# One projection stage of a hybrid transformer trunk: small loads issued at other places, and the third batch of triangular systems solved beside 12 token tiles of the second sweep

## The chip, the cores and the metric

The kernel runs on one core of one Trainium2 chip, as one launch. The metric is the device time of that launch in microseconds. Three executions of the kernel before took 3792.86, 3789.95 and 3793.18 us, median 3792.86 us. Names of engines in this text: PE is TensorE's matmul, PEld its weight load, DVE is VectorE, ACT is ScalarE, POOL is GpSimd, and SP is SyncE, whose instruction queue issues nearly all DMAs here.

## The reference, cut to what matters

One layer for 256 prompt tokens and 2048 latent tokens (18 tiles of 128 tokens together). The input `h` is normalised and modulated, and one projection of it feeds three groups of heads: A (attention with normalised and rotated q and k), B (a gated DeltaNet in chunks of 64 tokens, in both directions) and C (neighbourhood attention). Then follow an output projection and a SwiGLU FFN.

```python
def latent_mixer(h, ka_ctx, va_ctx, s_ctx, kc_ctx, vc_ctx, w_in, g_qk_a, ...):
    a_q, a_k, a_v, b_qkv, b_g, b_beta, b_alpha, c_q, c_k, c_v = split_projection(h @ w_in)
    qa = axial_rope(rmsnorm(a_q.reshape(b, L, A_HEADS, HEAD_DIM), g_qk_a[0]))
    ka = axial_rope(rmsnorm(a_k.reshape(b, L, A_KV_HEADS, HEAD_DIM), g_qk_a[1]))
    o_a = blocked_attention(qa, jnp.concatenate([ka, ka_ctx], axis=1), ...)
    q, k, v, beta, g = deltanet_prep(b_qkv, b_beta, b_alpha, conv_w, a_log, dt_bias)
    o_b, _ = bidir_delta(q, k, v, beta, g, ...)      # needs the triangular systems below
    ...
def gated_delta_chunked(q, k, v, g, beta, s0):       # one 64x64 system for each chunk and head
    ...
    sol = lax.linalg.triangular_solve(lmat + jnp.eye(CHUNK, dtype=lmat.dtype), rhs, left_side=True, lower=True, unit_diagonal=True)
```

`g = -exp(a_log) * softplus(b_alpha + dt_bias)`; `a_log` and `dt_bias` are 8 numbers each, `g_qk_a` is two rows of 64 numbers.

## The kernel before, in words

**Stages.** In the trace the order is: columns of B and the DeltaNet's short convolution (`phase_b`, up to about 308 us), then `phase_ac`, which has two sweeps over the 18 token tiles, then attention of group A from 826.7 us on (`group_a`), group C, the output projection and the FFN (up to 3788 us). `sweep(0, ...)` multiplies every token tile with three sets of weights for group C (q, k and v columns, 384 each), `sweep(1, ...)` with two sets for group A (320 each) and the last three tiles' v columns of C. A tile's product, `pso<-whi,hi` and its like on PE, is 24 matmuls, since each fp32 operand is split in two rounded parts (`hi` and `lo`, `whi` and `wlo`; `load_w` loads a set of weights in four chunks `wraw`, ACT rounds each to `whi` and DVE takes the rest, `wlo`). The token tiles `hi` and `lo` are read back from DRAM, 512 KB each for 128 tokens times 8 blocks.

**The second sweep's own work on DVE.** `qk_heads` normalises and rotates each tile's q and k: `qss`, a root on POOL (`qr5r`, `qr3r`), `zn`, then `zo` with the tables `cos` and `sin`; `gq` holds the two rows of `g_qk_a` on all 128 partitions. The keys go to DRAM (`ka`), come back four tiles at a time by `k_load` (tile `kd`), and are transposed by PE (`pt<-ident,kd`) and split by ACT and DVE (`KA<-pt`) in `k_dups`. `k_load(3)` and `k_load(4)` read the last six tiles; `k_dups(4)` is the last thing ahead of the scores of group A (`Sa<-KA,q`, then `mx`, the row maximum, on DVE).

**Background work.** `gates` makes `beta` and the decays, for which it loads `dt` and `al` (8 numbers, copied to 128 partitions). `preps` builds the systems. `solves` inverts them in five batches on DVE: each loads `sA` and `sB`, makes `sW<-sA,sB`, runs 76 pairs of a product `stmp<-sW` and a sum `sW<-stmp` (152 operations), and ends with `sC<-sW`, stored as `sysN` and `sysT`. `sA` and `sC` are the same buffer. Group A's recurrence needs three batches at its start, the others later. `Background.run(us)` emits pieces up to a credit of so many us of DVE work; in the second sweep it is called after each tile's columns with `SA`, in `group_a` at each turn of the scores with 2.0.

**What sets the order.** The kernel is emitted by a Tile scheduler that sorts each engine's instructions by priority and by its own model of time; `tc.high_priority(offset=HP)` moves what stands within it forward; an `InOrder` proxy (`self.pe`, and `self.sp` where `.on` is set) keeps program order. An engine then runs its list strictly in order, and SP too: a DMA that waits for its data holds up all DMAs behind it.

Of the kernel before, what the change touches and what calls it, by code (L numbers as in the profile page):

```python
# [7 lines left out]
F32 = mybir.dt.float32  # L8
# [3 lines left out]
ALU = mybir.AluOpType  # L12
# [47 lines left out]
class K:  # L60
    WQ = 0
    RA, NPE = 6, (8, 0, 0)
    INAC, ST = False, False
    SW, SA = (4.2, 1.8, 3.4), 0.8

    def __init__(self, tc, a, dbg=None, stop=99):
        self.tc = tc
# [214 lines left out]
    def phase_b(self):  # L282

        nc, a, tc = self.nc, self.a, self.tc
# [4 lines left out]
        with ExitStack() as es:  # L289
# [3 lines left out]
            wp = es.enter_context(tc.tile_pool(name="wp", bufs=1))  # L293
            wk = es.enter_context(tc.tile_pool(name="wk", bufs=2))
# [10 lines left out]
            nc.sync.dma_start(self.mask, a["masks"])  # L305
            self.mi = self.ctile("mi", [128, 2, 64])
            nc.sync.dma_start(self.mi, a["mi"])
            W = None
            zts = {}

# [20 lines left out]
            def conv(b):  # L331
                edges(b, True)
                edges(b, False)
                y = wk.tile([128, 6, BT], F32, tag="y", name="y", bufs=1)
                for f in range(6):
                    taps(b, f, y)
                conv_out(b, y)
# [19 lines left out]
            for b in range(NB):  # L357
                h = nxt
                if W is None:
                    W = [self.load_w(640, 384, wp, "a"), self.load_w(1024, 384, wp, "b"),  # L360
                         self.load_w(1408, 272, wp, "c")]
                if b + 1 < NB:
                    nxt = self.make_h(b + 1, self.load_x(b + 1, xin), hp, wk, pst)
                z = wk.tile([128, 6, BT + 2], F32, tag="zt", name="zt", bufs=3)
                zts[b] = z
                for f in range(6):
                    his, los = W[f // 3]
                    fs = slice(128 * (f % 3), 128 * (f % 3) + 128)
                    p = pso.tile([128, BT], F32, tag="pso", name="pso")
                    self.mm3(p, [x[:, fs] for x in his], [x[:, fs] for x in los],  # L370
                             [h[0][:, k, :] for k in range(KD)], [h[1][:, k, :] for k in range(KD)])
                    nc.scalar.activation(z[:, f, 1:1 + BT], p, AF.Copy)
                    if b == NB - 1:
                        if f == 0:
                            edges(b, True)
                            edges(b, False)
                            yl = wk.tile([128, 6, BT + 2], F32, tag="zt", name="yl", bufs=3)[:, :, 0:BT]
                        taps(b, f, yl)
                for i in range(3):
                    t = 3 * b + i  # L380
                    p = self.tokmm(h, i, 272, *W[2], pso)
                    o = wk.tile([128, 256], F32, tag="ev", name="ev", bufs=2)
                    nc.scalar.activation(o, p[:, :256], AF.Copy)
                    nc.vector.tensor_copy(self.ba[:, t, :], p[:, 256:272])
                    nc.sync.dma_start(self.bg_d[t], o)
                if b > 0:
                    conv(b - 1)
                if b in (1, 3):
                    self.mod_part(1 if b == 1 else 2, sb, xp, psm)
            conv_out(NB - 1, yl)  # L390

    def phase_ac(self, es_a, es_p, HB=3):

        nc, a, tc = self.nc, self.a, self.tc
# [8 lines left out]
        with ExitStack() as es:  # L403
            cst = es.enter_context(tc.tile_pool(name="pin_c", bufs=1))
            hp = es.enter_context(tc.tile_pool(name="hp2", bufs=HB))
            wp = es.enter_context(tc.tile_pool(name="wp2", bufs=1))
            wk = es.enter_context(tc.tile_pool(name="wk2", bufs=2))
# [28 lines left out]
            prep = Background(preps())  # L436
            HP = 1000
            self.bg = Background(solves())

            cos = cst.tile([128, NLAT, 32], F32, name="cos")  # L440
            sin = cst.tile([128, NLAT, 32], F32, name="sin")
            gq = cst.tile([128, 8, 64], F32, name="gq")
# [50 lines left out]

            def a_cols(n, t, h, W):
                p = self.tokmm(h, 0, 320, *W, pso)
                g = a_tile(n, t, p)
                next(g)
                a_flush()
                pend.append(g)
# [30 lines left out]
            def h_next():  # L530

                if seq:
                    x = seq.pop(0)
                    with tc.high_priority(offset=HP):
                        hs[x] = h_tile(x[1])

            def sweep(w, Ws, us, us2, us3, after=lambda t: None, mid=lambda t0, j, i: None):

                for t0, n0 in [(0, HB)] + [(t, 1) for t in range(HB, NT - HB)] + [(NT - HB, HB)]:
                    for j, (cols, n, W, tiles) in enumerate(Ws):  # L540
                        for i in range(n0):
                            end = j == max(k for k, x in enumerate(Ws) if t0 + i in x[3])
                            if t0 + i in tiles:
                                mid(t0, j, i)
                                with tc.high_priority(offset=HP):
                                    cols(n, t0 + i, hs[w, t0 + i], W)
                                if end:
                                    h_next()
                                prep.run(us)
                                self.bg.run(us2 if prep.left else us3)  # L550
                    with tc.high_priority(offset=HP):
                        after(t0)

# [1 line left out]
            self.sp.on = self.INAC  # L555
            self.st = nc.scalar if self.ST else nc.sync
            Wc = []
            for n in range(3):
                with tc.high_priority(offset=2 * HP if n == 0 else 0):
                    w = self.load_w(1680 + 384 * n, 384, wp, f"s{n}", ww=384, q=nc.scalar if n < self.WQ else None)  # L560
                Wc.append((c_cols, n, w, range(NT if n < 2 else NT - HB)))
                h_next()
            self.sp.dma_start(cos, a["cos"])
            self.sp.dma_start(sin, a["sin"])
            gsrc = a["g_qk_a"]
            self.sp.dma_start(gq[:, 0:6, :], gsrc[0, 0:1, :].unsqueeze(1).to_broadcast([128, 6, 64]))
            self.sp.dma_start(gq[:, 6:8, :], gsrc[0, 1:2, :].unsqueeze(1).to_broadcast([128, 2, 64]))
            nc.vector.tensor_scalar(gq[:, 0:6, :], gq[:, 0:6, :], 0.125, None, ALU.mult)
            sweep(0, Wc, *self.SW)
            prep.run(1e9)  # L570
            es2.close()
            wa = es.enter_context(tc.tile_pool(name="wa", bufs=2))
# [67 lines left out]
    def gates(self, wk, ps):  # L640
        nc, a = self.nc, self.a
# [8 lines left out]
        t8 = lambda n: wk.tile([128, NT, 8], F32, name=n, tag=n)  # L650
        v = nc.vector
        nc.scalar.activation(self.beta, self.ba[:, :, 0:8], AF.Sigmoid)
        dt = wk.tile([128, 8], F32, name="dt")
        al = wk.tile([128, 8], F32, name="al")
        self.sp.dma_start(dt, a["dt_bias"].rearrange("o d h -> o (d h)").to_broadcast([128, 8]))
        self.sp.dma_start(al, a["a_log"].rearrange("o d h -> o (d h)").to_broadcast([128, 8]))
        x, ax, e, u, d, m = [t8(n) for n in ("gx", "gax", "ge", "gu", "gd", "gm")]
        v.tensor_tensor(x, self.ba[:, :, 8:16], dt.unsqueeze(1).to_broadcast([128, NT, 8]), ALU.add)
        v.scalar_tensor_tensor(ax, x, -1.0, x, ALU.mult, ALU.max)
# [23 lines left out]
        q = ps.tile([128, 2, NT, 8], F32, tag="pg1", name="p_gl")  # L683
# [17 lines left out]
        for n, (t0, nt) in enumerate(((0, NLAT), (NLAT, NCTX))):  # L701
            w = 8 * nt
# [386 lines left out]
    def group_a(self):  # L1089
        nc, tc, a = self.nc, self.tc, self.a  # L1090
        self.EV = ()
        self.oa_d = [self.dtile(f"oa{t}", [128, 384]) for t in range(NT)]
        with ExitStack() as es:
            sp = es.enter_context(tc.tile_pool(name="A_p", bufs=2))
            tp = es.enter_context(tc.tile_pool(name="A_pt", bufs=4))
            wk = es.enter_context(tc.tile_pool(name="A_w", bufs=2))
# [74 lines left out]
            for g in range(len(groups)):  # L1171
# [4 lines left out]
                n = len(parts)  # L1176
# [15 lines left out]
                for pr in range(3):  # L1192
                    if g + 1 < len(groups):
                        if pr < 2:
                            t = groups[g + 1][pr]
# [4 lines left out]
                    for h2 in range(2):  # L1200
                        h = 2 * pr + h2
                        kv = h // 3
                        for qi in range(2):
# [35 lines left out]
                            if n > 1:  # L1239
                                nc.vector.tensor_reduce(sm[:, 3:4], sm[:, 0:n], AX.X, ALU.add)  # L1240
                            nc.vector.reciprocal(rs[:, qi, h2:h2 + 1], sm[:, 3:4] if n > 1 else sm[:, 0:1])
                            self.bg.run(2.0)
                            trs += turn(P, PT[h2], nk, qi)
                    if pvs:
                        late.append(pvs.pop())
# [313 lines left out]
    def phase_out(self):  # L1559
        nc, tc, a = self.nc, self.tc, self.a  # L1560
        v = nc.vector
        with ExitStack() as es:
            cst = es.enter_context(tc.tile_pool(name="o_c", bufs=1))
            wk = es.enter_context(tc.tile_pool(name="o_w", bufs=2))
# [40 lines left out]
            def rest(t):  # L1605

                zt.pop(t)
                x, m = xt.pop(t), mt.pop(t)
                self.residual(wk, m, x, gt[:, 0 if t < NLAT else 1, :])
                self.sp.dma_start(self.x1_d[t], x)  # L1610
                xn = self.raw() if t == NT - 1 else wk.tile([128, 1024], F32, tag="xn", name="xn", bufs=3)
                nt[t] = xn
                sq = wk.tile([128, 1024], BF16, tag="rjunk", name="sq2", bufs=1)
                s2 = wk.tile([128, 1], F32, tag="s2", name="s2")
                nc.scalar.activation(sq, x, AF.Square, accum_out=s2)
                r2 = self.rstd(wk, s2, 1, 1.0 / D, "o2")
                v.tensor_scalar(xn, x, r2, None, ALU.mult)
# [537 lines left out]
```

## Time and profile before

| what | value |
|---|---|
| median of three runs | 3792.86 us |
| the profiled execution's own time, its span | 3790.19 us, 3788.4 us |
| mean granted TensorE clock | 0.982 |
| busy: PE, DVE, ACT, POOL | 95%, 63%, 45%, 16% |
| start of the first sweep: 300 to 382 us | PE busy 56.49 of 82.00 us |
| second sweep and its end: 625 to 823 us | PE busy 168.27 of 198.00 us, DVE 150.22 us |
| group A, first 12 units of scores: 827.0 to 925.2 us | PE busy 88.53 of 98.20 us, DVE 85.99 us |
| group A, third 12 units: 1023.7 to 1122.2 us | PE busy 97.19 of 98.50 us, DVE 55.77 us |

A unit of group A is one block of scores (`Sa`, `Sb`, `Sc`) with its row maximum, softmax and products. The profiled execution lies 2.67 us under the median. Times in the text are microseconds from the start of the span. In rows with several engines, each has its busy time and, in brackets, its number of instructions. A row of the timeline is start, duration, engine, line, operation, output and inputs, shape, count, and in brackets the engine's idle time ahead of it and what ended that.

### The profile page before, as it was taken

What the parts mean: (1) busy time and instruction counts of PE and PEld (TensorE: products, weight loads), DVE (VectorE), ACT (ScalarE), POOL (GpSimd) and SP (SyncE); (2) the same over time, 40 slices, a digit from 0 to 9 for tenths busy, and PEclk for the clock granted to TensorE, in tenths of its full rate; (3) what the DMA queues carried; (4) which work ended last, traced back from release to release, by engine and by line L of the source; (5) the groups of instructions that cost most, each with busy time, mean ns of one, the idle gap of its engine ahead of it and who ended that gap; (6) DMA issues with size and microseconds to landing.
All of it is one profiled execution on the core that took longest, in us unless ns stands there. A gap on an engine that the chain in (4) does not pass through costs nothing.

```text
span 3788.4 us, 64737 instructions
## 1 busy us (share of the span) xinstructions
PE 3601.8 (95%) x24526; PEld 3157.9 (83%) x24526; DVE 2398.9 (63%) x5030; ACT 1718.5 (45%) x3533; POOL 590.5 (16%) x859
## 2 busy tenths in 40 slices
PE   8997999979999999989999989999999999999999
PEld 5886888966777777768877879999999999788887
DVE  4784477689755555558874667778778777322433
ACT  4223222226666666656775653344334333322321
POOL 0002321630000000000003411111111111000121
PEclk9998999989999999999999999999999999999999
DMA  7555877842111121155324753333334333534653
GB/s 267 207 203 178 255 221 227 212 115 55 44 52 52 53 53 51 48 140 164 99 65 161 232 162 102 98 103 118 102 97 121 103 97 95 189 110 130 202 181 129
DMA packets 647496, 501.14 MB, mean 132 GB/s; under 512 B 253505, under 2 KB 576944, under 8 KB 644624
## 3 DMA queue, kind: packets, MB, share of 16 engines
q1 hardware_dynamic: 644400, 493.40, 43.3%
q8 instruction: 193, 3.16, 0.4%
q10 hardware_dynamic: 2624, 3.55, 0.3%
q14 instruction: 119, 0.97, 0.1%
q0 software_dynamic: 160, 0.05, 0.0%
HBM read 348.14 MB, written 148.73 MB: 131 GB/s over the span
## 4 chain that ended last, share of the span: by engine, by line
PE 74%; DVE 11%; ACT 4%; POOL 4%; DMA 3%; issue 3%; SPq 1%; ACTq 0%; DVEq 0%; POOLq 0%
PE pd L37 15%; PE Y L37 11%; PE pso L37 8%; PE X L37 7%; PE Z L37 7%; PE pt L37 7%; PE po L37 6%; PE rx L37 3%; DVE stmp L843 2%; PE Sa L37 2%; PE Sb L37 2%; PE S L37 2%; DVE mx L1220 2%; PE m L37 1%; DVE sW L844 1%
## 5 line engine op out<-in xcount | busy, mean ns | idle before, releaser
L1034 ACT ACTIVATE PT<-pt 128x512 f32<-128x512 f32 (+1 forms) x600 | 332.4, 554 | 257.4 <-PE pt L37 250.6
L37 PE MATMUL Y<-hop,raw 128*128 128x384 f32 x1788 | 341.5, 340 | 12.7 <-DVE u L1874 9.3
L37 PEld LDWEIGHTS Y<-hop,raw 128*128 128x128 f32 x1788 | 317.8, 190 | 14.1 <-DVE u L1874 10.0
L37 PE MATMUL po<-PT,V 128*64 128x256 f32 (+1 forms) x3072 | 313.3, 340 | 2.2 <-ACT PT L1034 1.9
L37 PE MATMUL pso<-whi,hi 128*128 128x384 f32 (+2 forms) x864 | 286.6, 332 | 27.5 <-ACT whi L255 15.0
L37 PE MATMUL pt<-ident,P 128*128 128x128 f32 x1752 | 285.2, 280 | 14.7 <-ACT PT L1034 7.9
L37 PE MATMUL pso<-whi,lo 128*128 128x384 f32 (+2 forms) x864 | 280.9, 325 | 8.0 <-DMA lo<-hl 8.0
L37 PE MATMUL pso<-wlo,hi 128*128 128x384 f32 (+2 forms) x864 | 280.8, 325 | 1.6 <-DVE wlo L256 1.6
L37 PEld LDWEIGHTS pt<-ident,P 128*128 128x128 f32 x1752 | 200.4, 141 | 94.0 <-ACT PT L1034 35.4
L37 PEld LDWEIGHTS po<-PT,V 128*64 128x64 f32 x3072 | 180.1, 136 | 79.1 <-issue 33.8
L37 PE MATMUL Z<-hop,raw 128*128 128x384 f32 x1188 | 224.1, 337 | 0.0
L37 PE MATMUL X<-hop,raw 128*128 128x384 f32 x1176 | 222.9, 338 | 0.0
L1742 DVE TENSOR_TENSOR raw<-S,raw 128x512 fp32r<-128x512 f32 x198 | 146.8, 742 | 115.5 <-ACT raw L1741 110.5
L37 PEld LDWEIGHTS Z<-hop,raw 128*128 128x128 f32 x1188 | 209.6, 188 | 0.0
L37 PEld LDWEIGHTS X<-hop,raw 128*128 128x128 f32 x1176 | 208.4, 188 | 0.0
L1885 POOL TENSOR_TENSOR o<-sg,p 128x384 f32<-128x384 f32 x66 | 91.7, 1390 | 733.5 <-DVE p L1884 406.1
L1741 ACT ACTIVATE raw<-S 128x512 fp32r<-128x512 f32 x198 | 124.9, 631 | 177.9 <-PE X L37 68.2
L37 PEld LDWEIGHTS pso<-whi,hi 128*128 128x128 f32 x864 | 166.7, 193 | 31.8 <-ACT whi L255 16.5
L37 PE MATMUL pd<-wd,ao 128*128 128x512 f32 x756 | 185.5, 394 | 0.0
L37 PE MATMUL pd<-wd,hop 128*128 128x512 f32 x756 | 183.0, 392 | 0.0
L971 POOL TENSOR_TENSOR rSe<-rS,eh 64x128 f32<-64x128 f32 x144 | 55.0, 401 | 811.0 <-DVE rS L1003 780.2
L1741 ACT ACTIVATE raw<-wr 128x512 fp32r<-128x512 f32 x160 | 100.9, 631 | 168.1 <-PE Z L37 79.1
(346 smaller groups left out, 8336.0 us busy)
## 6 DMA issues: line engine op xcount, KB each, us to landing
hr<-a SPq DMA_DIRECT2D x72, 704.0 KB, 4.5
wr<-in_w_gu_dram SPq DMA_DIRECT2D x66, 512.0 KB, 4.0
wr<-in_w_gu_dram SPq DMA_DIRECT2D x132, 256.0 KB, 3.0
a<-o SPq DMA_DIRECT2D x396, 64.0 KB, 1.6
wm<-in_w_mod_dram SPq DMA_DIRECT2D x48, 512.0 KB, 4.3
hi<-hh SPq DMA_DIRECT2D x36, 512.0 KB, 5.1
lo<-hl SPq DMA_DIRECT2D x36, 512.0 KB, 6.3
st<-ptk SPq DMA_DIRECT2D x18, 768.0 KB, 4.1
```

What stands on the lines that cost most here:

```text
L37: r = f(*x, **kw)
L843: v.tensor_tensor(tv, M[:n, c0:c1, c0:i], M[:n, c0:i, i].unsqueeze(1).to_broadcast([n, m, k]), ALU.mult)
L844: v.tensor_reduce(M[:n, c0:c1, i], tv, AX.X, ALU.add)
L971: nc.gpsimd.tensor_tensor(Se[hh[x], d], S[hh[x], d, :, hh[x]], e.unsqueeze(2).to_broadcast([64, 2, 64]), ALU.mult)
L1034: self.nc.scalar.activation(out, p, AF.Copy)
L1220: nc.vector.tensor_reduce(mx[:, i:i + 1], S[:, :hi_ - lo_], AX.X, ALU.max)
L1741: self.nc.scalar.activation(hi, raw, AF.Copy)
L1742: self.nc.vector.tensor_tensor(lo, raw, hi.bitcast(F32), ALU.subtract)
L1885: nc.gpsimd.tensor_tensor(o[:, 0], sg, p1, ALU.mult)
```

## The change

Five edits:

1. The loads of `dt` and `al` are issued in `phase_b` after block 1, not in `gates`.
2. In the program the loads of `cos`, `sin` and `gq`, and the multiplication of `gq`, stand in a callback of the first sweep at tiles 8 and 10, no longer ahead of the sweep.
3. At the head of the first sweep token tiles and weights are issued on SP in program order: tile 0, weights 0, tiles 1 and 2, weights 1, weights 2.
4. In the second sweep the background is run only up to tile 11, with 1.15 us of credit at a call, not 0.8, and at high priority; in `group_a` the credit is 1.1, not 2.0.
5. In the output projection a 128x1 tile shares the tag of another.

```diff
-    SW, SA = (4.2, 1.8, 3.4), 0.8
+    SW, SA = (4.2, 1.8, 3.4), 1.15
...
+            self.dt, self.al = self.ctile("dt", [128, 8]), self.ctile("al", [128, 8])
...
+                if b == 1:
+                    nc.sync.dma_start(self.dt, a["dt_bias"].rearrange("o d h -> o (d h)").to_broadcast([128, 8]))
+                    nc.sync.dma_start(self.al, a["a_log"].rearrange("o d h -> o (d h)").to_broadcast([128, 8]))
...
-                                self.bg.run(us2 if prep.left else us3)
+                                if w == 0:
+                                    self.bg.run(us2 if prep.left else us3)
+                                elif t0 < 12:
+                                    with tc.high_priority(offset=HP):
+                                        self.bg.run(us3)
...
+            self.sp.on = True
             for n in range(3):
+                if n < 2:
+                    h_next()
                 with tc.high_priority(offset=2 * HP if n == 0 else 0):
-                    w = self.load_w(1680 + 384 * n, 384, wp, f"s{n}", ww=384, q=nc.scalar if n < self.WQ else None)
+                    w = self.load_w(1680 + 384 * n, 384, wp, f"s{n}", ww=384)
                 Wc.append((c_cols, n, w, range(NT if n < 2 else NT - HB)))
-                h_next()
-            self.sp.dma_start(cos, a["cos"])
-            self.sp.dma_start(sin, a["sin"])
-            gsrc = a["g_qk_a"]
-            self.sp.dma_start(gq[:, 0:6, :], gsrc[0, 0:1, :].unsqueeze(1).to_broadcast([128, 6, 64]))
-            self.sp.dma_start(gq[:, 6:8, :], gsrc[0, 1:2, :].unsqueeze(1).to_broadcast([128, 2, 64]))
-            nc.vector.tensor_scalar(gq[:, 0:6, :], gq[:, 0:6, :], 0.125, None, ALU.mult)
-            sweep(0, Wc, *self.SW)
+                if n == 0:
+                    h_next()
+            self.sp.on = self.INAC
+
+            def rotary(t):
+                if t == 8:
+                    self.sp.dma_start(cos, a["cos"])
+                    self.sp.dma_start(sin, a["sin"])
+                if t == 10:
+                    ...
+            sweep(0, Wc, *self.SW, rotary)
...
-                            self.bg.run(2.0)
+                            self.bg.run(1.1)
```

The change shifts line numbers: `stmp` and `sW` of the solves are L843 and L844 before, L859 and L860 after; `KA` is L1023 before and L1039 after. PE's list of instructions is the same in both kernels. Three places move.

**SP, at the end of `phase_b` and the head of the first sweep.** `bg` and `y` are stores of `phase_b`, `cq` is a store of the first sweep's first products. Before:

```order
L385 DMA bg_184<-ev 128x256
L37 DMA wraw<-in_w_in_dram 128x2x384 x3
L37 DMA hi<-hh_156 128x8x128
L37 DMA wraw<-in_w_in_dram 128x2x384
L37 DMA hi<-hh_156 128x8x128 x2
L37 DMA lo<-hl_162 128x8x128 x3
L385 DMA bg_185<-ev 128x256
L354 DMA y_198<-ye 128x768
```

The broadcasts stood about ten rows further down, between the second set's weights:

```order
L37 DMA gq<-in_g_qk_a_dram 128x6x64
L523 DMA cq<-ev 768x1x64
L37 DMA gq<-in_g_qk_a_dram 128x2x64
L37 DMA wraw<-in_w_in_dram 128x2x384
L37 DMA dt<-in_dt_bias_dram 128x8
L37 DMA al<-in_a_log_dram 128x8
L37 DMA wraw<-in_w_in_dram 128x2x384 x2
```

After, from the same store of `bg` on:

```order
L386 DMA bg_184<-ev 128x256
L37 DMA cos<-in_cos_dram 128x512
L37 DMA sin<-in_sin_dram 128x512
L37 DMA gq<-in_g_qk_a_dram 128x6x64
L37 DMA gq<-in_g_qk_a_dram 128x2x64
L386 DMA bg_185<-ev 128x256
L355 DMA y_198<-ye 128x768
L355 DMA y_199<-ye 128x768
L355 DMA y_200<-ye 128x768
L37 DMA hi<-hh_156 128x8x128
L37 DMA lo<-hl_162 128x8x128
L37 DMA wraw<-in_w_in_dram 128x2x384 x3
```

So the scheduler has put the loads of `cos`, `sin` and `gq` ahead of the first tile and the first weights, though the program writes them into the sweep. Of the second set's four chunks three now stand behind the second `cq` and the fourth behind the third `cq`. On DVE the multiplication of `gq` stands ahead of the first `wlo`.

**DVE, where the second sweep ends.** Before, the third batch's last row, the key splits of `k_dups(3)` and `k_dups(4)`, the first row maxima of group A, and then the fourth batch's start:

```order
L844 TENSOR_REDUCE sW<-stmp 128x7
L847 COPY sC<-sW 128x1024
L1023 TENSOR_TENSOR KA_6616<-pt,KA_6616 64x512 x2
L1023 TENSOR_TENSOR KA_6617<-pt,KA_6617 64x256 x2
L1220 TENSOR_REDUCE mx<-Sa 128x1
L1220 TENSOR_REDUCE mx<-Sb 128x1
L1220 TENSOR_REDUCE mx<-Sc 128x1
L1224 TENSOR_REDUCE mx<-mx 128x1
L833 TENSOR_TENSOR sW<-sA,sB 128x1024
```

After, the third batch ends ahead of the last tiles' rotation, and the fourth batch starts right behind that:

```order
L478 TENSOR_TENSOR zo<-zo,zu 128x5x32
L475 TENSOR_TENSOR zo<-zn,cos 128x5x32
L476 TENSOR_TENSOR zo<-zn,sin 128x5x32
L478 TENSOR_TENSOR zo<-zo,zu 128x5x32
L849 TENSOR_TENSOR sW<-sA,sB 128x1024
L850 MEMSET sW 128x32
L859 TENSOR_TENSOR stmp<-sW 128x1
L860 TENSOR_REDUCE sW<-stmp 128x1
```

and the first of the key splits stand 67 of its operations later:

```order
L859 TENSOR_TENSOR stmp<-sW 128x160
L860 TENSOR_REDUCE sW<-stmp 128x3
L1039 TENSOR_TENSOR KA_6616<-pt,KA_6616 64x512
L860 TENSOR_REDUCE sW<-stmp 128x8
L1039 TENSOR_TENSOR KA_6616<-pt,KA_6616 64x512
L859 TENSOR_TENSOR stmp<-sW 128x96
```

Between these two and the `KA` of `k_dups(4)` stand 25 operations of the batch (one between the two, 24 behind), and about ten more ahead of the first `mx`; the other 50 come in group A's first units, with the fifth batch behind them at about its old place.

**SP, at the same place.** Before, `k_load(3)` and `k_load(4)` were issued between the stores of the last tiles:

```order
L37 DMA qa<-zn 128x64
L37 DMA kd<-ka 128x8x64 x2
L508 DMA va<-ev 128x128
L37 DMA ka<-zn 128x128
L37 DMA out_dram<-zn 128x128
```

After, both stand behind all of those stores, the third batch's `sysN` and `sysT`, and the loads of the fourth batch's `sA`:

```order
L867 DMA sysN_116<-sW 64x1024
L866 DMA sysT_110<-sC 128x1024
L37 DMA qa<-zo 128x64 x2
L37 DMA ka<-zo 128x128
L37 DMA qa<-zn 128x320
L845 DMA sA<-low_101 64x32x32 x2
L37 DMA qa<-zn 128x320
```

The two `kd<-ka` pairs follow seven rows further down, behind `qa<-zo` and `ka<-zo` of the last tile.

More of the change, by code (lines that the diff above doesn't have):

```diff
@@ L557, in phase_ac @@
             Wc = []
+            self.sp.on = True
             for n in range(3):
+                if n < 2:
+                    h_next()
                 with tc.high_priority(offset=2 * HP if n == 0 else 0):
-                    w = self.load_w(1680 + 384 * n, 384, wp, f"s{n}", ww=384, q=nc.scalar if n < self.WQ else None)
+                    w = self.load_w(1680 + 384 * n, 384, wp, f"s{n}", ww=384)
                 Wc.append((c_cols, n, w, range(NT if n < 2 else NT - HB)))
-                h_next()
-            self.sp.dma_start(cos, a["cos"])
-            self.sp.dma_start(sin, a["sin"])
-            gsrc = a["g_qk_a"]
-            self.sp.dma_start(gq[:, 0:6, :], gsrc[0, 0:1, :].unsqueeze(1).to_broadcast([128, 6, 64]))
-            self.sp.dma_start(gq[:, 6:8, :], gsrc[0, 1:2, :].unsqueeze(1).to_broadcast([128, 2, 64]))
-            nc.vector.tensor_scalar(gq[:, 0:6, :], gq[:, 0:6, :], 0.125, None, ALU.mult)
-            sweep(0, Wc, *self.SW)
+                if n == 0:
[6 more added lines that the diff above has]
+                if t == 10:
+                    gsrc = a["g_qk_a"]
+                    self.sp.dma_start(gq[:, 0:6, :], gsrc[0, 0:1, :].unsqueeze(1).to_broadcast([128, 6, 64]))
+                    self.sp.dma_start(gq[:, 6:8, :], gsrc[0, 1:2, :].unsqueeze(1).to_broadcast([128, 2, 64]))
+                    nc.vector.tensor_scalar(gq[:, 0:6, :], gq[:, 0:6, :], 0.125, None, ALU.mult)
+            sweep(0, Wc, *self.SW, rotary)
             prep.run(1e9)
@@ L652, in gates @@
         nc.scalar.activation(self.beta, self.ba[:, :, 0:8], AF.Sigmoid)
[L653 to L656, printed above, removed]
+        dt, al = self.dt, self.al
         x, ax, e, u, d, m = [t8(n) for n in ("gx", "gax", "ge", "gu", "gd", "gm")]
@@ L1613, in rest @@
                 sq = wk.tile([128, 1024], BF16, tag="rjunk", name="sq2", bufs=1)
-                s2 = wk.tile([128, 1], F32, tag="s2", name="s2")
+                s2 = wk.tile([128, 1], F32, tag="rss", name="s2")
                 nc.scalar.activation(sq, x, AF.Square, accum_out=s2)
```

## The prediction, made before the changed kernel ran

> **What bounds the kernel now.** I read the page's head first, then the windows by stage, and within the stages that the change touches the timeline and the waits.
>
> ```profile
> span 3788.4 us, 64737 instructions
> PE 3601.8 (95%) x24526; PEld 3157.9 (83%) x24526; DVE 2398.9 (63%) x5030; ACT 1718.5 (45%) x3533; POOL 590.5 (16%) x859
> ```
>
> PE is the bound over the whole, so only places where PE idles or runs at a low clock can give time back. The windows (length, busy time of each engine, clock, DMA share, GB/s) show where that is:
>
> ```profile
> 300.00:382.00 82.00, 56.49 (x306) 50.34 (x305) 34.23 (x77) 28.98 (x52) 23.33 (x54) 0.81 0.67 200
> 340.00:360.00 20.00, 6.74 (x16) 4.60 (x16) 5.07 (x14) 7.21 (x14) 0.00 (x0) 0.50 0.54 170
> 625.00:823.00 198.00, 168.27 (x1076) 164.70 (x1074) 150.22 (x503) 47.59 (x127) 92.86 (x168) 0.95 0.66 173
> 827.00:925.20 98.20, 88.53 (x710) 64.53 (x711) 85.99 (x281) 65.89 (x137) 5.02 (x12) 0.96 0.34 80
> 925.20:1023.70 98.50, 94.37 (x928) 71.53 (x925) 79.73 (x247) 65.46 (x137) 6.35 (x16) 1.00 0.20 53
> 1023.70:1122.20 98.50, 97.19 (x956) 74.48 (x955) 55.77 (x121) 67.42 (x140) 6.06 (x16) 1.00 0.19 51
> ```
>
> The first sweep's head loses 25 us of PE, and between 340 and 360 the clock is halved. The second sweep loses 30. Group A's first 24 units lose 8.7 and 2.8 us of PE against the third dozen, which has few solves (DVE 55.77).
>
> **Edits 1 to 3: the loads at the first sweep's head.** Here the timeline of PE, ACT and SP shows one stall and its cause:
>
> ```profile
> 322.26 0.69 PE L37 MATMUL pso<-whi,lo 128*128 128x384 f32 x1 [4.67 <-DMA lo<-hl]
> 352.46 0.69 PE L37 MATMUL pso<-whi,hi 128*128 128x384 f32 x1 [12.61 <-ACT whi L255]
> 374.37 1.01 PE L37 MATMUL p_gc<-g,mask 128*128 128x72 f32 x8
> 332.41 0.49 ACT L522 ACTIVATE ev<-pso 128x384 f32<-128x384 f32 x1 [3.61 <-PE pso L37]
> 336.57 0.49 ACT L522 ACTIVATE ev<-pso 128x384 f32<-128x384 f32 x1 [3.67 <-PE pso L37]
> 351.88 0.94 ACT L255 ACTIVATE whi<-wraw 128x384 fp32r<-128x384 f32 x2 [13.41 <-DMA wraw<-in_w_in_dram]
> 303.78 2.97 SPq L385 DMA_DIRECT2D bg<-ev  x2
> 339.38 8.58 SPq L37 DMA_DIRECT2D al<-in_a_log_dram  x1
> 348.01 1.47 SPq L37 DMA_DIRECT2D wraw<-in_w_in_dram  x2
> ```
>
> The products start in earnest at 322.26, a tile takes 4.16 us (336.57 less 332.41), and the second set stops PE for 12.61 us since its chunk landed late. What was late is told by the DMAs' landing (KB, us from issue to landing; window 335 to 340) and by what moved between 340 and 344:
>
> ```profile
> wraw<-in_w_in_dram SPq DMA_DIRECT2D x1, 384.0 KB, 13.5
> sin<-in_sin_dram SPq DMA_DIRECT2D x1, 256.0 KB, 4.1
> gq<-in_g_qk_a_dram SPq DMA_DIRECT2D x1, 192.0 KB, 14.5
> DMA packets 285, 0.07 MB, mean 18 GB/s; under 512 B 285, under 2 KB 285, under 8 KB 285
> ```
>
> The broadcast `gq` takes 14.5 us, though `sin`, as many bytes as both its parts, takes 4.1. Meanwhile only small packets move, at 18 GB/s, and the weights behind it take 13.5. `al` held SP for 8.58 us more, until 348.01.
>
> In the new order `gq` is issued at the end of `phase_b` instead, behind the `bg` store that ends at 306.75 (303.78 + 2.97). Add `cos` and `sin`, half a us each: `gq` issues at 307.7 and lands 14.5 us later, at 322.2. All that was moved past it waits: `bg`, three `y`, then the first `hi`, `lo` and chunk, some 2.7 MB. Taking the rate at which the same queue ran afterwards, 0.27 to 0.38 MB a us, that is 7 to 10 us more:
>
> ```profile
> DMA packets 1706, 1.08 MB, mean 269 GB/s; under 512 B 1163, under 2 KB 1702, under 8 KB 1705
> ```
>
> That row is 348 to 352, while the backlog was restarting, so I take the upper rate, an estimate. The first product starts at 330, 8 us later than 322.26. After that the first set's three tiles run through: 12.5 us plus 2 for a cold clock gives 344.5. The second set's first three chunks are issued behind the second `cq` (341) and land by 346.5; the fourth stands behind the third `cq` (345), lands at 350 and is rounded by 350.7. So the second set starts at 346.5, stalls a few us once, and ends its third tile at 360.5; the third set's first tile ends at 364.6. Before, that tile ended at 374.4, where PE goes on to `p_gc`. Gain 9.8, **taken as 10**. If the backlog also drains at 0.27, 3 us go; if the fourth chunk and the rounding are late by another 4, 3 are left; if `gq` delays nothing that was not late anyway, 15. So 3 to 15. A pass in which DMA (share 0.67 over the head) rather than PE is the bound would give part of it back later; I cover that with the low end.
>
> The small loads themselves: `dt` and `al` are now queued in `phase_b`, among its loads of modulation weights, and the exponential of `al` moves there too, with two more table loads on ACT. One of these in the trace:
>
> ```profile
> 353.68 1.28 ACT L661 ACT_TABLE_LOAD   x1 [0.86 <-DVE gax L659]
> ```
>
> Two of 1.28 us on an engine that is 45% busy: 0, at most 2.6 if a `y` waits for ACT. Later nothing waits for `al` any more; that is part of the gain above. The shared tag (edit 5) costs nothing, as it renames a 128x1 buffer.
>
> By the Trainium skill (DMA: Bandwidth & Descriptors, "Why a DMA increments its semaphore by 16 and not by 1") a load whose slowest dimension is 128 on both sides is spread over 16 engines, which would make `gq` as quick as `sin`. The 14.5 and 18 GB/s above speak against it; by the page the first gain would be some 18 and the whole forecast 8 us lower.
>
> **Edit 4: the second sweep's end.** The waits of PE there (us in total, times, longest) and the rows at its end:
>
> ```profile
> PE pt L37 <- DVE KA L1023: 10.3, 1, 10.3
> 751.57 2.41 DVE L833 TENSOR_TENSOR sW<-sA,sB 128x1024 f32<-128x1024 f32 x1
> 821.88 1.03 DVE L847 COPY sC<-sW 128x1024 f32<-128x1024 f32 x1
> 822.94 1.30 DVE L1023 TENSOR_TENSOR KA<-pt,KA 64x512 fp32r<-64x512 f32 x2
> 823.69 1.11 PE L37 MATMUL pt<-ident,kd 128*128 128x128 f32 x4 [10.26 <-DVE KA L1023]
> 826.71 2.04 PE L37 MATMUL Sa<-KA,q 128*128 128x512 f32 x4 [1.90 <-DVE KA L1023]
> DVE zn L456 <- POOL qr5r L91: 6.0, 5, 1.4
> DVE zn L456 <- POOL qr3r L91: 4.1, 5, 1.0
> ```
>
> DVE is the bound: the third batch and the rotations end at 822.9, and PE has waited 10.26 us for `KA` by then. From there to the first scores it is 3.8 us. In the new order DVE has the same rows up to this point, but the third batch ends earlier among them. The point moves by the 10 of the head, and by what is saved of the 10.1 us that `zn` waits for POOL in this stretch, since more batch rows now stand between; I take 4 (0 to 6). So the rotations end at 808.9.
>
> Then comes what is new: the start of the fourth batch, 67 of its operations, two `KA`, 25 more, two `KA`. Their price is that of the third batch's first 68 (35 products and 33 sums) and next 23 (11 and 12), grouped by line:
>
> ```profile
> 754.00:784.00 30.00, 8.79 (x35) 0.88 0.57 150
> 754.00:784.00 30.00, 6.16 (x33) 0.88 0.57 150
> 784.00:794.80 10.80, 4.02 (x11) 0.86 0.13 39
> 784.00:794.80 10.80, 2.80 (x12) 0.86 0.13 39
> ```
>
> 68 take 14.95, so 67 take 14.7; 25 take 25/23 of 6.82, 7.4. With `sW` 2.41, `KA` 2 x 0.65 and 2 x 0.43 and the step to PE that is 14.7 + 7.4 + 2.4 + 1.3 + 0.9 + 0.2 = 26.9. `sA` is issued only after `sysN` and `sysT` have left its buffer and after a rotated store, and took 4.1 us to land in this stretch; that starts the batch about 1.5 later: 28.4, against 3.8 before. The late `kd` loads cost nothing beside it: a `ka` store lands in 3.1 and `kd` in 5.7 or less, PE has 8 transposes and one tile of 4.2 to do, so the keys would be ready 14 us after the rotations. That is the floor of this term, if the batch cost nothing:
>
> ```profile
> kd<-ka SPq DMA_DIRECT2D x8, 256.0 KB, 5.7
> ka<-zo SPq DMA_DIRECT2D x16, 64.0 KB, 3.1
> sA<-low SPq DMA_DIRECT2D x4, 256.0 KB, 4.1
> ```
>
> So the first scores start at 808.9 + 28.4 = 837.3, 10.6 later than 826.71; between 14 and 30 behind the rotations, by the floor and by a slow `sW` start.
>
> What is given back: 102 of 152 operations are then done ahead of the first `mx`. The batch's work was in group A's first units, where DVE is the bound once the first scores are there (length, PE, PEld, DVE):
>
> ```profile
> 827.00:833.70 6.70, 3.92 (x11) 2.84 (x10) 2.94 (x4) 1.29 (x3) 1.83 (x4) 0.67 1.00 196
> 841.30:848.80 7.50, 5.46 (x31) 3.76 (x31) 7.33 (x32) 5.83 (x13) 0.00 (x0) 1.00 0.21 55
> ```
>
> DVE needs 55.77 for a dozen units without batches, so 26 us less of batch leaves PE as the bound there. But PE can only regain its own idle time, 8.7 in that dozen, of which 2.8 is the first unit's start-up, and 2.8 in the next, which the lower credit leaves as it is. I take 5 (2 to 9).
>
> **Sum**, against the profiled execution of 3790.19 us: head -10, POOL waits -4, junction 28.4 - 3.8 = +24.6, group A -5, together +5.6. Against the median, 2.67 above that execution, it gives 3792.86 + 5.6 = 3798.5.
>
> **The rivals.** Faster: `gq`'s delay is swallowed because `bg` and `y` had to leave anyway (head -15), and DVE's relief regains all of group A's early idle time (-9); with -6 and 14.7 + 7.4 - 3.8 + 4.8 = +23.1 this gives -7, and with the keys ready behind a quicker batch a few more: 3783. For it speaks that the fourth batch's work is not new, only early; against it, that PE has nothing to do while it runs. It decides once the first scores start before 831.
>
> Slower: the broadcast ahead of the first weights moves the stall rather than removes it. If the first `pso<-whi,hi` after `phase_b` starts later than 336, the head gives 3; then -3 - 3 + 26.2 - 4 is +16, 3809. For it speaks that SP issued nothing for 8.58 us while such packets were queued; against it, that only one stall is left where there were two.
>
> The change doesn't do what it says: the third batch starts on DVE where it did, and the loads are moved nearer to the first weights. If DVE's list merely exchanges idle time, gain and loss cancel: 3792.
>
> The skill's rule holds for a broadcast that starts on an idle queue (by rows: lands like `sin`, 4.1): the head gives 18, the sum -2.4, 3790.
>
> **How the numbers follow.** About 0.2% or 7.6 us is what a measurement of this kernel can tell from no change: 3785.3 and 3800.4 are the bounds. My forecast case has 0.38, its own range 3791 to 3804: 0.28 same, 0.10 slower. The slower rival 0.30: 0.25 slower, 0.05 same. The faster rival 0.20: 0.18 faster, 0.02 same. No effect 0.07 (0.02 faster, 0.05 same), the rule 0.05 (0.02 faster, 0.03 same). Together faster 0.22, same 0.43, slower 0.35. The range from 3780 to 3811 leaves out a tenth on each side.
>
> **What would show it.** In the profile after: `gq` landing near 322 and the first product of the sweep at about 330; no wait above 5 us for `whi` around 345, and the clock not halved for 20 us; the fourth batch's `sW<-sA,sB` near 810, and PE waiting over 20 us for `KA` before `Sa` at about 837; then a first dozen of units with PE busy at 92 or more of its window. I am wrong if PE starts the sweep by 324, or if `Sa` starts before 828: either would turn the sign. A rest of the span, from unit 24 on, that differs by more than 3 us would mean something that I have not seen.

## The result, and the profile after

The changed kernel takes 3812.43 us (median of four runs, 3811.57 to 3815.18) against 3792.17 us before (four runs): 20.3 us longer, ratio 1.0053 with a 95% interval of 1.004 to 1.0065. It is slower, and 1.4 us above the top of the range. The page's head, as in the prediction:

```profile
span 3809.8 us, 64711 instructions
PE 3610.0 (95%) x24526; PEld 3163.9 (83%) x24526; DVE 2397.4 (63%) x5030; ACT 1721.4 (45%) x3535; POOL 589.2 (15%) x859
```

DVE has the same work as before. PE's 8 us more come with the same number of matmuls and a lower granted clock (0.978 in the mean, 0.982 before). The same windows as before (length, busy time of PE, PEld, DVE, ACT, POOL, clock, DMA share, GB/s); group A's first dozen units now starts at 849.4:

```profile
320.00:340.00 20.00, 10.80 (x46) 9.55 (x47) 6.21 (x13) 4.24 (x9) 0.00 (x0) 0.67 1.01 292
340.00:360.00 20.00, 15.96 (x76) 14.23 (x75) 10.21 (x27) 10.90 (x21) 5.23 (x5) 0.91 0.90 275
625.00:823.00 198.00, 166.72 (x1025) 162.44 (x1023) 143.38 (x490) 44.22 (x118) 94.62 (x168) 0.91 0.65 168
823.00:850.00 27.00, 8.72 (x37) 8.21 (x38) 23.23 (x105) 2.46 (x5) 3.50 (x12) 0.66 0.63 149
849.40:947.40 98.00, 90.76 (x723) 66.63 (x724) 80.97 (x249) 67.89 (x141) 3.70 (x8) 0.93 0.23 56
```

The hole of 340 to 360 is smaller, but there is a new one at 320 to 340, and PE is busy 8.72 of the 27 us ahead of group A. The head first, from the timelines of PE, ACT and SP (an SPq row is a DMA that SP issues) and the DMAs' landing (KB, us):

```profile
321.37 0.69 PE L37 MATMUL pst<-ident,yl 128*128 128x128 f32 x2 [9.11 <-DVE es L354]
328.94 0.69 PE L37 MATMUL pso<-whi,hi 128*128 128x384 f32 x1 [6.88 <-ACT whi L255]
347.08 0.44 PE L37 MATMUL pso<-whi,hi 128*128 128x384 f32 x1 [1.94 <-ACT whi L255]
370.36 0.47 PE L37 MATMUL pso<-wlo,hi 128*128 128x384 f32 x1 [2.18 <-DVE wlo L256]
371.91 0.32 PE L37 MATMUL p_gc<-g,mask 128*128 128x72 f32 x1
353.06 0.94 ACT L255 ACTIVATE whi<-wraw 128x384 fp32r<-128x384 f32 x2 [1.81 <-DMA wraw<-in_w_in_dram]
312.28 8.51 SPq L37 DMA_DIRECT2D lo<-hl  x1
348.12 5.10 SPq L37 DMA_DIRECT2D wraw<-in_w_in_dram  x3
gq<-in_g_qk_a_dram SPq DMA_DIRECT2D x1, 64.0 KB, 12.0
```

The broadcast was issued at 308.0 and landed at 320.5; SP stood 8.51 us on one load behind it, and the first product starts at 328.94. The third set's first tile ends at 371.9, against 374.4: 2.5 us are left of the head's gain. Then the end of the second sweep, where the rest is lost. Waits of PE from 625 to 860 (total, times, longest), the DVE, ACT and SP rows on the way to the first scores:

```profile
PE pt L37 <- DVE sW L860: 13.5, 1, 13.5
PE pso L37 <- ACT zn L453: 10.3, 2, 8.4
PE Sa L37 <- DVE KA L1039: 8.0, 1, 8.0
808.02 0.44 ACT L453 ACTIVATE zn<-pso 128x320 f32<-128x320 f32 x1 [17.47 <-DVE stmp L859]
809.25 1.08 DVE L863 COPY sC<-sW 128x1024 f32<-128x1024 f32 x1
811.19 0.26 DVE L478 TENSOR_TENSOR zo<-zo,zu 128x96 f32<-128x96 f32 x1
812.77 0.45 SPq L37 DMA_DIRECT2D ka<-zo  x1
819.31 0.32 SPq L37 DMA_DIRECT2D qa<-zn  x1
821.36 0.31 DVE L478 TENSOR_TENSOR zo<-zo,zu 128x160 f32<-128x160 f32 x1
825.84 1.23 DVE L849 TENSOR_TENSOR sW<-sA,sB 128x1024 f32<-128x1024 f32 x1 [4.17 <-DMA qa<-zn]
826.44 0.44 SPq L37 DMA_DIRECT2D ka<-zo  x1
828.67 2.47 SPq L37 DMA_DIRECT2D kd<-ka  x4
849.51 2.05 PE L37 MATMUL Sa<-KA,q 128*128 128x512 f32 x4 [7.96 <-DVE KA L1039]
```

The first scores start at 849.5, 22.8 us later than before. The last row of the third batch starts at 809.25 rather than 821.88, as the order said. But look at the keys: their last rotation on DVE (`zo` of 96 columns) starts at 811.19, SP issues nothing between 813.2 and 819.31, where a `qa<-zn` store waits, the last `ka` store leaves at 826.44 and `kd` is loaded behind it. The same rows of the kernel before, and its last rotation of a q tile:

```profile
791.55 0.25 DVE L474 TENSOR_TENSOR zo<-zo,zu 128x96 f32<-128x96 f32 x1
801.77 0.43 SPq L37 DMA_DIRECT2D ka<-zn  x1
803.54 0.93 SPq L37 DMA_DIRECT2D kd<-ka  x2
808.41 0.63 DVE L474 TENSOR_TENSOR zo<-zo,zu 128x160 f32<-128x160 f32 x1 [0.43 <-POOL zu L470]
```

There the keys were on their way 25 us earlier, hidden beside the end of the third batch. On DVE the batch and the rotations have changed places: before, the last rotation ends at 809.0 and the batch at 822.9; now the batch ends at 810.3 and the last rotation at 821.7. Of the 24.7 us by which the last `ka` store leaves later, about 10 are the later last key (the last `zn` of a key tile ends at 801.38 before, the last rotation of keys at 811.45 now); the other 14.6 are the wait in SP's list.

### The profile page after: what moved, and what is told of

It is laid out like the page before. It is cut to its first block, busy times and chain, and to the rows that moved or that the text cites. A ratio compares the mean times of both kernels' runs of the same rounds, so it can differ in the third digit from the quotient of the medians.

```text
span 3809.8 us, 64711 instructions
## 1 busy us (share of the span) xinstructions
PE 3610.0 (95%) x24526; PEld 3163.9 (83%) x24526; DVE 2397.4 (63%) x5030; ACT 1721.4 (45%) x3535; POOL 589.2 (15%) x859
## 4 chain that ended last, share of the span: by engine, by line
PE 75%; DVE 11%; ACT 4%; DMA 3%; issue 3%; POOL 3%; SPq 1%; ACTq 0%; POOLq 0%; DVEq 0%
PE pd L37 15%; PE Y L37 10%; PE pso L37 9%; PE X L37 7%; PE Z L37 7%; PE pt L37 7%; PE po L37 6%; PE rx L37 3%; PE m L37 2%; DVE stmp L859 2%; PE Sa L37 2%; PE Sb L37 2%; PE S L37 2%; DVE mx L1236 2%; DVE sW L860 1%
```

## The experiments

Sixteen kernels ran. Three theories were open after the result: J, that the fourth batch's operations ahead of the last key splits make the loss; H, that the broadcast at the head does; and, from e4 on, P, that the priority of the third batch does, since it puts the last key rotations behind it. "First scores" is the start of the first `Sa` in the run's profile.

**Which edit.** e1 undoes edit 4 in the changed kernel, e2 makes edit 4 alone in the kernel before:

```diff
-    SW, SA = (4.2, 1.8, 3.4), 1.15          # e1; e2 the other way round
+    SW, SA = (4.2, 1.8, 3.4), 0.8
...
-                                if w == 0:
-                                    self.bg.run(us2 if prep.left else us3)
-                                elif t0 < 12:
-                                    with tc.high_priority(offset=HP):
-                                        self.bg.run(us3)
+                                self.bg.run(us2 if prep.left else us3)
...
-                            self.bg.run(1.1)
+                            self.bg.run(2.0)
```

> The changed kernel with edit 4 undone: background of the second sweep and of group A as before, loads as changed. Theory J (the loss is made where the second sweep ends, by the fourth batch's operations ahead of the last key splits): the first scores start within 4 us of the 826.7 of before, the time is 3786 to 3794. Rival H (the broadcast ahead of the first weights is what costs): most of the 20 us stays, 3805 or more.

> The kernel before with edit 4 alone. Theory J: the first scores start about 25 us later than before, near 852, group A gives about 6 back, and the time is 3810 to 3816. Rival H: 3790 to 3796.

e1: 3789.22 us, ratio 0.999 (0.9981 to 0.9998), first scores at 825.4. e2: 3812.67 us, ratio 1.0051 (1.0037 to 1.0064), first scores at 852.1. Edit 4 makes the whole loss; the loads give 3 us, which the interval barely tells from nothing. H falls.

**What the broadcast costs.** e3 loads `gq` as two rows of 64 in the kernel before and spreads them on DVE; e7 does the same in e1; e11 keeps the 1024 pieces of 256 bytes but takes them from 128 rows of another tensor, so it scales the heads by other numbers and only its time is of use:

```diff
-            self.sp.dma_start(gq[:, 0:6, :], gsrc[0, 0:1, :].unsqueeze(1).to_broadcast([128, 6, 64]))
-            self.sp.dma_start(gq[:, 6:8, :], gsrc[0, 1:2, :].unsqueeze(1).to_broadcast([128, 2, 64]))
-            nc.vector.tensor_scalar(gq[:, 0:6, :], gq[:, 0:6, :], 0.125, None, ALU.mult)
+            g2 = cst.tile([128, 2, 64], F32, name="g2")                          # e3, e7
+            self.sp.dma_start(g2, gsrc[0:1].to_broadcast([128, 2, 64]))
+            nc.vector.tensor_scalar(gq[:, 0:6, :], g2[:, 0:1, :].to_broadcast([128, 6, 64]), 0.125, None, ALU.mult)
+            nc.vector.tensor_copy(gq[:, 6:8, :], g2[:, 1:2, :].to_broadcast([128, 2, 64]))
...
+            xs = a["x_sample"][0, 0:128, :].rearrange("p (c d) -> p c d", d=128)[:, :, 0:64]   # e11
+            self.sp.dma_start(gq[:, 0:6, :], xs[:, 0:6, :])
+            self.sp.dma_start(gq[:, 6:8, :], xs[:, 6:8, :])
```

> The kernel before with gq loaded as one row of 64 numbers for q and one for k on each partition (128 packets of 512 bytes or 256 of 256, 64 KB) and spread to 8 heads by DVE, all at the same place. If the broadcast's 14.5 us is the number of its packets at about 71 a us, it lands in 4 us or less, the second set's wait for whi falls from 12.6 us to 4 or less, and the time falls by 6 to 10 us, to 3783 to 3787. Rival: the chunk is late because SP was held elsewhere (al, or a full queue), and the wait stays above 8 us and the time within 3 us of before.

> The changed kernel with edit 4 undone and gq loaded as 64 KB instead of 256: cos, sin and this load stand ahead of the first weights. If the broadcast's length was what delayed the first product to 329, it starts by 324, and the third set's first tile ends by 364 (374.4 before, 371.9 after); the time is 3781 to 3787. If the order of SP (weights behind cq and py) is what ate the gain, the second set still stalls for 4 us or more and the time is 3786 to 3792.

> The kernel before with gq filled from 128 different rows of x_sample (other numbers, so the rotated heads are scaled otherwise): as many pieces of 256 bytes at the same place, but none read twice. If the number of pieces sets the time, gq still lands in 12 us or more and the second set waits 11 us or more for whi. If reading one row 128 times is what is slow, it lands in 6 us or less and the wait falls below 5.

e3: 3782.89 us, ratio 0.9979 (0.997 to 0.9988). e7: 3779.5 us, ratio 0.9966 (0.9955 to 0.9976), 1.5 us under the range that I gave. e11, one run: 3783.89 us. The DMAs' landing in e3 (`g`) and in e11 (`gq`), PE in e3 and in e7:

```profile
g<-in_g_qk_a_dram SPq DMA_DIRECT2D x1, 64.0 KB, 3.7
gq<-in_x_sample_dram SPq DMA_DIRECT2D x1, 192.0 KB, 4.3
339.98 0.69 PE L37 MATMUL pso<-whi,hi 128*128 128x384 f32 x1 [2.47 <-ACT whi L255]
362.27 1.00 PE L37 MATMUL p_gc<-g,mask 128*128 128x72 f32 x8
322.19 0.69 PE L37 MATMUL pso<-whi,hi 128*128 128x384 f32 x1 [8.88 <-ACT whi L255]
361.88 1.01 PE L37 MATMUL p_gc<-g,mask 128*128 128x72 f32 x8
```

With the narrow load the wait of 12.61 us falls to 2.47. The third set's first tile ends 12.1 us earlier in the old order (374.4 to 362.3) and 10.0 in the new one (371.9 to 361.9), so the length of this load was worth more than its place. e11 narrows down what made it long: as many pieces from different rows land in 4.3 us, not 14.5, so the number of pieces is not it. The reading of one row again and again is left; e11 changes the tensor along with the rows, and no run separates the two.

**The last steps to the first scores.** e4 keeps the third batch where the changed kernel has it in the program, but holds the fourth back until group A (`later` is set there); e5 leaves the fourth batch's products and sums out of the changed kernel, e6 out of the kernel before; e9 issues the last `ka` stores and `kd` loads from POOL; e10 is e5 and e9 together:

```diff
-                    while self.ready < need:                                     # e4
+                    while self.ready < need or (self.solved == 3 and not self.later):
                         yield 1000.0
+            v.tensor_copy(W[0:1, 0:1], self.KA[1][0:1, 1, 255:256].bitcast(F32)) # e4, fourth batch only
...
+                if (d, bi) != (0, 1):                                            # e5, e6, e10
                     v.tensor_tensor(tv, M[:n, c0:c1, c0:i], ...)
                     v.tensor_reduce(M[:n, c0:c1, i], tv, AX.X, ALU.add)
...
-                self.sp.dma_start(self.ka_d[:, t, :], ...)                       # e9, e10; kd of 3 and 4 likewise
+                (nc.gpsimd if t >= 12 else self.sp).dma_start(self.ka_d[:, t, :], ...)
```

> The changed kernel, but the fourth batch is emitted only in group A and its first operation reads the last key split, so that on DVE it starts behind it (as before), while the third batch stays beside the first tiles at high priority. Theory J: the first scores start 8 to 15 us behind the last rotation, at 815 to 830 rather than 849, and the time is 3785 to 3797. Rival R (the third batch's high priority delays the rotations, ACT zn and so PE by itself): the last rotation ends no earlier than 821, the scores not before 832, and the time is 3798 to 3806.

> The changed kernel with the fourth batch's 152 products and sums left out (its loads, its first and its last row stay), so that nothing stands between the rotations and the key splits on DVE but sW and sC. In the changed kernel the first scores started 27.8 us behind the last rotation. If those operations are what held them, they start about 14 us behind it (stores of ka, load of kd, one tile and the splits); if the late kd loads are as long a chain by themselves, 20 us or more behind it.

> The kernel before with the same operations left out: the first scores start where they did (826 to 827), and what group A, up to the first scores of group C, is shorter by is the most that moving the whole fourth batch out of it can give. From the first dozen's idle PE time: 5 to 9 us.

> The changed kernel with three kinds of DMA issued by POOL instead of SP: the stores of ka from tile 12 on, and the loads of kd for the last six tiles. On DVE the scheduler then puts the key splits of k_dups(3) right behind sW of the fourth batch and those of k_dups(4) some 23 operations later. If SP's order is what made the keys late (the last ka store stood behind stores of qa and cv for 15 us), kd lands by 821, the first scores start at 831 to 837 rather than 849.5, and the time is 3796 to 3803. If the fourth batch's operations or a late end of the rotations hold them, they start after 843 and the time is above 3807.

> The same with the fourth batch's products and sums left out as well. If two chains of about equal length ended at the first scores (SP's keys, 23 us behind the rotations; DVE's batch, 28), taking away both leaves 8 to 12 us behind the last rotation, near 831, while taking away the operations alone left 23.0.

e4: 3800.77 us, ratio 1.0021 (1.0012 to 1.003). Here the scheduler started the third batch earlier still (718.7), and PE shows a price of that before any fourth batch:

```profile
779.28 0.64 PE L37 MATMUL pso<-whi,hi 128*128 128x320 f32 x1 [13.47 <-ACT zn L454]
842.45 1.17 PE L37 MATMUL Sa<-KA,q 128*128 128x512 f32 x4 [1.90 <-DVE KA L1043]
```

That is what P says and J does not. But e4 is 11.7 us under the changed kernel, and since both batches moved it can't say which of them gave that. e5 (one run, 3805.2 us) starts its scores at 846.0, with `kd` as what PE waits for; its last rotation ends at 823.0, so 23.0 us are left of the changed kernel's 27.8 without any of those operations:

```profile
835.58 0.66 PE L37 MATMUL pt<-ident,kd 128*128 128x128 f32 x2 [14.36 <-DMA kd<-ka]
846.01 1.48 PE L37 MATMUL Sa<-KA,q 128*128 128x512 f32 x4 [2.73 <-DVE KA L1040]
```

e6 (one run, 3783.77 us): first scores at 827.0, and from there to the first scores of group C 818.2 us, against 825.9 before: 7.7 is all that the fourth batch costs group A. Taken together, e5 is 21.4 us longer than e6: without any of the fourth batch's operations on either side the loss is as large as with them. That speaks against J more plainly than any row, though each is one run. e9: 3806.18 us, ratio 1.0039 (1.0026 to 1.0051), first scores at 842.9, far from the 831 to 837 that I gave. e10 (one run, 3801.89 us): 842.5, and not the 831 expected. With both suspects gone the scores are still 16 us late. But neither run removes SP's wait alone: in the new order DVE rotates the last keys at 819.9 in e9 and 820.4 in e10, some 9 us later than in the changed kernel, behind two `zn` that wait for POOL. In e10 the last `ka` store then leaves POOL, the load follows, and then PE (rows of DVE, POOL and PE):

```profile
820.36 0.45 DVE L478 TENSOR_TENSOR zo<-zo,zu 128x96 f32<-128x96 f32 x1 [0.76 <-POOL zu L474]
822.00 0.58 POOL L515 DMA_DIRECT2D ka<-zo  x1
825.87 1.88 POOL L601 DMA_DIRECT2D kd<-ka  x2 [1.18 <-DMA ka<-zo]
832.92 1.94 PE L37 MATMUL pt<-ident,kd 128*128 128x128 f32 x8 [10.71 <-DMA kd<-ka]
842.53 1.17 PE L37 MATMUL Sa<-KA,q 128*128 128x512 f32 x4 [1.91 <-DVE KA L1040]
```

From the last `ka` store to the first scores it is 20.5 us by itself: 3.9 to the load's issue, 7 to PE, 9.6 for transposes, one tile and splits. J falls as the main cause: what decides is when the last keys are stored. In all 18 profiles the first scores start 18.0 to 25.2 us behind the last `ka` store, whether that leaves at 788.6 (e16) or at 829.3 (e2); in the kernel before, where the third batch ends last, it is 24.9. How much of its delay would stay if the late rotation or SP's order were mended alone, no run shows.

**The priority.** e13 puts the background of the second sweep below the rotations, e14 gives it no priority; both keep the amounts of edit 4:

```diff
-                                    with tc.high_priority(offset=HP):            # HP is 1000
+                                    with tc.high_priority(offset=400):           # e13
                                         self.bg.run(us3)
```

> The changed kernel with the second sweep's background at priority offset 400 instead of 1000 (the rotations and the columns have 1000); the amounts of work are as changed. If the third batch's priority over the last key rotations makes the loss, those rotations end about where they did before (last ka store at 800 to 805), the first scores start at 820 to 829, and the time is 3782 to 3793. If the amount or place of background work makes it, the first scores start after 838 and the time is above 3803.

> The changed kernel with the background at normal priority, amounts as changed. Priority theory: as the changed loads alone (3789.2), 3785 to 3793. Amount theory: above 3803.

e13: 3790.98 us, ratio 1.0001 (0.999 to 1.0011). e14: 3783.54 us, ratio 0.9978 (0.9969 to 0.9987), first scores at 825.1, the time 1.5 us under the range that I gave. The rows of e13 (DVE, SP, PE):

```profile
789.77 0.25 DVE L478 TENSOR_TENSOR zo<-zo,zu 128x96 f32<-128x96 f32 x1
800.29 0.43 SPq L37 DMA_DIRECT2D ka<-zn  x1
802.06 0.93 SPq L37 DMA_DIRECT2D kd<-ka  x2
821.11 2.04 PE L37 MATMUL Sa<-KA,q 128*128 128x512 f32 x4 [1.90 <-DVE KA L1039]
```

One number, the priority, takes 21 us off the changed kernel: the keys are rotated at 789.8 again, and the first scores start 28 us earlier than in it. P holds. (In e13 the fourth batch starts behind the first scores again, at 827.7, so this run alone would not tell P from J; e5 and e6 do.)

**Faster versions.** e8 is the kernel before with the narrow `gq`, edit 1 and edit 5. e12 is the changed kernel with the narrow `gq` and e9's queue; e15 is e8 with edit 4 at e13's priority; e16 is e8 with the lower credit in group A alone.

> The kernel before with edit 1 (dt and al in phase_b), edit 5 and the narrow gq, all else as before. The second set's wait for whi, 2.5 us with the narrow gq alone, falls to 1.5 or less; the time is 3779 to 3784, 1 to 3 us below the narrow gq alone. Rival: the two more table loads or the loads in phase_b give that back, 3783 to 3786.

> The changed kernel with the narrow gq and the keys on POOL's queue. The first product of the sweep starts at 322 to 324, the first scores at 820 to 828, and the time is 3776 to 3788; whether it is below the 3776.5 of the kernel before with the narrow gq and edit 1 tells whether edit 4 is worth anything once its two costs are gone. I expect it within 8 us above.

> The kernel before with the narrow gq, edits 1 and 5 (3776.5 so far) and edit 4 at offset 400. If the third batch really moves earlier without delaying the keys, PE's wait of 10 us for the key splits shrinks, the first scores start before 812 and the time is 3768 to 3775. If the batch only changes places with other rows on a busy DVE, 3774 to 3780.

> The kernel before with the narrow gq, edits 1 and 5 (3776.5) and only the credit in group A changed from 2.0 to 1.1. If the lower credit is worth the 5 us between the two kernels above, the stretch from the first scores of group A to the first of group C (825.9 us before) is 5 us or more shorter and the time is 3769 to 3774; if they were scatter, it is 3774 to 3780.

e8: 3776.53 us, ratio 0.9962 (0.9949 to 0.9974), the fastest median: 16 us below the kernel before, and 2.5 under the range that I gave. e12: 3796.83 us, ratio 1.0013 (1.0004 to 1.0022), first scores at 830.3, both outside what I gave: the priority stayed in, and its last `ka` store leaves at 808.1, against 789.4 in e8. e15: 3780.05 us, ratio 0.9968 (0.9956 to 0.998), first scores at 817.5 against 814.5 in e8; e16: 3778.12 us, ratio 0.9961 (0.9948 to 0.9975). Neither the earlier third batch nor the lower credit adds to e8 anything that these runs can tell; that e14 came out 6 us below e1 is not settled by them.

## Why the prediction was wrong, step by step

I forecast +5.6 us and measured +20.3. The profiled executions differ by 21.4 in span: -1.2 up to the end of the rotations and the third batch, +24.0 for the junction behind it, -7.0 in group A, +5.6 in the rest. I had -14, +24.6, -5 and 0. Term by term:

- **The head, -10 forecast, -2.5 measured.** Landing of `gq` (322.2 forecast, 320.5), first product (330; 328.9) and the second set's start (346.5; 347.1) were right. The step that failed is the stretch from there to the end of the third set's first tile: 18.1 us forecast (346.5 to 364.6), 24.8 measured. I priced its four tiles at 4.16 each; in the kernel before the same four took 21.9 (352.46 to 374.37), at a granted clock of 0.82. The rest is mostly waits: the fourth chunk was to be "rounded by 350.7", but SP took 5.10 us over three loads at 348.12, the rounding ran at 353.06, and the third set met the same spacing again (2.18 us at 370.36). My low end of 3 named this lateness. By the end of the group A columns (799.73 before, 799.76 after) nothing was left of it; the second sweep has new waits for `kd` (3.7 us) and for `zn` (8.4 us just behind).
- **The rotations' end at 808.9: measured 821.67.** This is the step with the largest error, 12.8 us. I took DVE's rows up to that point as the same work in another order, and moved their common end (822.9) by the 10 of the head and 4 of POOL. The head's gain was gone by then, `zn` waits for POOL 10.6 us in the same stretch against 10.1 (2.30, 1.20 and 1.34 us in the tail), and the exchange was not neutral: batch rows, which nothing waits for, came ahead of rotations, which ACT (17.47 us idle), PE and the keys wait for.
- **The junction, 28.4 forecast, 27.8 measured.** The chain on DVE that I priced is what released the first scores (PE waited 7.96 us for `KA`), but that its length agreed is partly luck: `sW` started 4.2 us behind the rotations instead of 1.5 and ran 1.23 instead of 2.41, and the 67 operations took 12.8 us (827.28 to 840.1), not 14.7: rows of the two lines overlap, and I added them (the 68 rows of the third batch together are 13.71 us, not 14.95). What failed is the other chain: I called the late `kd` loads free, with a floor of 14. e5 has 23.0 without the operations, so they add 4.8. The floor was sized from the landing of each DMA and left out the second transposition, its splits and the lower clock (0.66 from 823 to 850), and the store's place on SP: the key tile rotated at 811.19 left at 826.44, behind stores of `qa` and `cv` and the loads of `sA`.
- **Group A, -5 forecast, -7.0 measured** (825.9 us from its first scores to those of group C before, 818.9 after); e6 bounds it at 7.7. Right in size, though PE is busy 90.76 us in the first dozen units, not the 92 that I gave as its sign.
- **The rest of the span, 0 forecast**, is 5.6 longer in this profile (15.8 late at group C's first scores, 21.4 at the end). In e1 the same stretch is 2.0 longer, in e2 6.3, in e8 2.3 shorter. It stays open, with a lead: in the eleven kernels with the lower credit in group A it is 0.6 to 6.5 longer, in the six others from 2.3 shorter to 2.9 longer, one profile each. In the profile after, 4.0 of the 5.6 lie between the first and the last scores of group C, where PE waits longer for a load of group C's q (`qd<-cq`; before, then after):

```profile
PE pt L37 <- DMA qd<-cq: 5.7, 3, 3.1
PE pt L37 <- DMA qd<-cq: 9.6, 4, 4.7
```

Of the rivals the slower one named the right time (3809) for a reason that did not occur: the first product did not start after 336. The rule of the Trainium skill that I weighed (DMA: Bandwidth & Descriptors, "Why a DMA increments its semaphore by 16 and not by 1") spoke of the spread over engines by shape. e11 has the same shape on both sides and lands in 4.3 us, which agrees with that rule, though no view here counts the engines. The conclusion that I drew from it, that `gq` would be as quick as `sin`, fails on its 14.5 us.

## What to carry to other kernels

When background work is moved forward at the priority of the main work, ask what in the main work starts a long chain of stores, loads and transposes, and keep that ahead: here the last keys take 20 us from store to scores, free while a batch ran beside them and exposed behind it. Count such a chain to its last consumer, from the rows of the place where it ran alone, and look at what its DMAs stand behind on their queue. And before a slow load is moved, find out why it is slow: made a quarter as large it was worth 9 us, moved to another place 3.

## What the runs showed of the hardware that was not expected

A load that copies a short row of DRAM many times can be slow by its source. 768 pieces of 256 bytes from one row of `g_qk_a` landed 14.5 us after their issue in the kernel before (18 GB/s while little else moved); as many from 128 rows of another tensor took 4.3 us (e11), and 64 KB from the two rows of `g_qk_a` 3.7 us (e3). It does not hold for every copied row: the kernel also spreads two rows of 4096 bytes over 128 partitions, and those land in 4.2 us each (issued at 1980.9 in the kernel before):

```profile
gt<-gate_d SPq DMA_DIRECT2D x2, 512.0 KB, 4.2
```

What stands behind the slow load lands late: in the changed kernel `lo` 15.0 us after its issue, which itself held SP for 8.5 us.
